# Residual products of a decoder layer as two matmuls over 64 rows of the array each

## The chip, the cores and the metric

One core of one Trainium2 chip runs the whole layer in one launch. The metric is the device time of one execution in microseconds (us).

## The reference

A hybrid decoder layer on 256 tokens of width 2048, batch 1, depth 1, all in float32. Three times a product with a weight matrix is added to the residual stream h:

```python
hn = rmsnorm(h, norm_mix_w[l])
q, k, v, g_ret, xr, yr, g_a, g_b = jnp.split(hn @ w_in[l], offsets, axis=-1)
...
merged = (jax.nn.sigmoid(g_a) * (ret_out @ w_proj_ret[l])
          + jax.nn.sigmoid(g_b) * (rnn_out @ w_proj_rnn[l]))
h = h + merged @ w_mix_out[l]
hn = rmsnorm(h, norm_xa_w[l])
mem_n = rmsnorm(mem, norm_mem_w[l])
h = h + memory_cross_attention(hn, mem_n, xa_w_q[l], xa_w_k[l], xa_w_v[l], xa_w_o[l])
hn = rmsnorm(h, norm_ffn_w[l])
h = h + conv_gated_ffn(hn, ffn_w_up[l], ffn_conv_w[l], ffn_conv_b[l], ffn_w_down[l])
return rmsnorm(h, final_norm_w)
```

memory_cross_attention ends in `o @ w_o` (2048 x 2048), conv_gated_ffn in `(silu(gate) * val) @ w_down` (5632 x 2048).

## The kernel before

Every weight matrix is streamed from HBM once, in chunks of 512 x 512 (KC = 4 k-tiles of 128 rows, BW = 512 columns). A chunk is loaded into `raw` by SyncE's queue, cast to a rounded float32r part `hi` by ScalarE (L210), and its remainder `lo` = raw - hi is formed by VectorE (L211). Activations are split into a high and a low part in the same way (`s` tiles: columns 0 to 255 hold the high part of 256 tokens, 256 to 511 the low part). A product is then three float32r matmuls: high x hi, low x hi, high x lo.

There are two forms of product. gemm_t keeps the weights in the array and streams the activations; its result has features on the partitions (L266). gemm_n keeps 128 tokens of the activations in the array and streams 512 columns of a weight part; its result has tokens on the partitions, `acc[:, tt, :]` with tt = 0, 1 for the two row tiles of 128 tokens (products_n, L276 to L278). One chunk in gemm_n is 2 row tiles x 4 k-tiles x 3 = 24 matmuls, the 12 of tt = 0 first. A block of 512 output columns with 2048 rows of weights has four chunks.

The accumulators come from a pool `pm` of three tiles, each of two PSUM banks (128 x 2 x 512 float32); gemm_t takes two of them, gemm_n one. Small results (transposes, scores, attention) use a second pool `px` of two one-bank tiles.

`plan` lists all products in order, and `chunks` fetches each chunk AHEAD = 2 chunks before use. Work between products is hung on this sequence by `later(n, fn)`, which runs fn n + 1 chunks further on; so transposes of the residual (`turn`, L306) stand between the chunks of the next block. The order on each engine is fixed when the program is built. Work inside `tc.high_priority(URGENT)` is put earlier in it.

The residual products are `residual` (L709; w_mix_out and xa_w_o, four blocks each) and `down` (L838; w_down in three parts of 4, 4 and 3 blocks of hidden features, for each of them four blocks of output columns). Each adds its accumulator to `hrow[b]`, the residual with tokens on the partitions, in one VectorE instruction of 128 x 1024, and ScalarE then squares the rows for the next rmsnorm (`squares`, L725). The last block of the last part of `down` has a form of its own, with two accumulators and halves of 256 columns.

Of the kernel before, what the change touches and what calls it, by code (L numbers as in the profile page):

```python
# [16 lines left out]
P = 128  # L17
D = 2048
S = 256
NT = D // P  # L20
# [7 lines left out]
BW = 512  # L28
KC = 4
KH = 2  # L30
# [4 lines left out]
URGENT = 5  # L35
# [29 lines left out]
def hybrid_layer(  # L65
# [25 lines left out]
    act, dve, pe, pool, sp = nc.scalar, nc.vector, nc.tensor, nc.gpsimd, nc.sync  # L91
# [11 lines left out]
    def nm(s):  # L103
        count[0] += 1
        return f"{s}_{count[0]}"

    def big(shape, dt=F32, s="b"):
        return bp.tile(shape, dt, tag="big", name=nm(s))
# [4 lines left out]
    def acc():  # L113
        return pm.tile([P, 2, BW], F32, tag="acc", name=nm("acc"))
# [48 lines left out]
    b0 = 0  # L163
# [57 lines left out]
    def later(n, fn):  # L221

        pending.append((step[0] + n + 1, fn))

    def chunks(nk, w, row, c):

        w_, row_, nk_, c_ = plan[gemms[0]]
        assert (row_, nk_, c_) == (row, nk, c) and w_.tensor is w.tensor, (gemms[0], row, nk, c)
        gemms[0] += 1
        for k in range(0, nk, KC):  # L230
            prefetch(1)
            (r_, c_), parts = ahead.pop(0)
            assert (r_, c_) == (row + k * P, c)
            prefetch(AHEAD)
            yield k, parts
            step[0] += 1
            due = [p for p in pending if p[0] <= step[0]]
            pending[:] = [p for p in pending if p[0] > step[0]]
            for _, fn in due:
                fn()  # L240

    def gemm_t(w, row, st, nk, col):

        accs = [acc(), acc()]
        first = gemms[0] == 0
        phase = 0
        for k0, parts in chunks(nk, w, row, col):
            last = k0 + KC >= nk
            for pr in range(2):
                if first and k0 == 0:  # L250
                    runs = [[(t, kk, j) for t in (0, 1)] for kk in range(KC) for j in range(2)]
                else:
                    if k0 == 0:
                        phase = 0
                    elif last:
                        phase = 1
                    runs = [[(t, kk, j) for j in range(2) for kk in range(KC)] for t in (phase, 1 - phase)]
                    phase = 1 - phase
                for t, kk, j in (r for run in runs for r in run):
                    k = k0 + kk  # L260
                    sx = st[k // 2][:, k % 2, :]
                    part = parts[kk // KH][t][:, kk % KH, (2 * pr + j) * P : (2 * pr + j + 1) * P]
                    a = accs[pr][:, j, :]
                    if t == 1:
                        a, sx = a[:, S:BW], sx[:, 0:S]
                    pe.matmul(  # L266
                        a, part, sx, start=k == 0 and t == 0, stop=k == nk - 1 and t == 0, skip_group_check=True
                    )
                if pr == 0 and not last:
                    st[(k0 + KC) // 2 + 1]  # L270
        return accs

    def products_n(o, sx, hi, lo, tt, start, stop):
        h = sx[:, tt * P : (tt + 1) * P]
        l = sx[:, S + tt * P : S + (tt + 1) * P]
        pe.matmul(o, h, hi, start=start, stop=False)  # L276
        pe.matmul(o, l, hi, start=False, stop=False)  # L277
        pe.matmul(o, h, lo, start=False, stop=stop)  # L278

    def gemm_n(w, row, st, nk, col):  # L280

        a = acc()
        for k0, parts in chunks(nk, w, row, col):
            for tt in range(2):
                for kk in range(KC):
                    k = k0 + kk
                    hi, lo = (t[:, kk % KH, :] for t in parts[kk // KH])
                    products_n(a[:, tt, :], st[k // 2][:, k % 2, :], hi, lo, tt, k == 0, k == nk - 1)
        return a

    def product(o, l, r, start, stop):

        for i, (a, b) in enumerate(((l[0], r[0]), (l[0], r[1]), (l[1], r[0]))):
            pe.matmul(o, a, b, start=start and i == 0, stop=stop and i == 2, skip_group_check=True)  # L294
# [87 lines left out]
    def rsqrt_small(ap, n, scale, eps):  # L382
        v = sp_.tile([P, n], F32, tag="rv", bufs=4, name=nm("rv"))
        dve.tensor_scalar(out=v, in0=ap, scalar1=scale, scalar2=eps, op0=ALU.mult, op1=ALU.add)
        o = sp_.tile([P, n], F32, tag="ro", bufs=5, name=nm("ro"))
        pool.tensor_tensor(out=o, in0=v, in1=mhalf[:, 0:n], op=ALU.pow)
        return o
# [158 lines left out]
    for g in range(2):  # L546
        dec = big([P, 4, S], s="dec")
        vs, turned = [], []
        for b, o in enumerate((O_Q, O_K)):
            a = qacc if g == b == 0 else gemm_t(w0, 0, xs, NT, o + g * BW)  # L550
# [13 lines left out]
        for b in range(2):  # L564
            a = gemm_n(w0, 0, xs, NT, O_G + g * 1024 + b * BW)
            t = big([P, 2, BW], s="gate")
# [70 lines left out]
    for b in range(4):  # L637
# [4 lines left out]
        for pr, a in enumerate(gemm_t(w0, 0, xs, NT, O_XR + b * BW)):  # L642
            z = scaled(a, "xz")
            for j in range(2):
                t = 4 * b + 2 * pr + j
# [56 lines left out]
    def residual(w, st, out, wcol, steps=None):  # L702

        ss = sp_.tile([P, 2, 4], F32, tag="ss0", name=nm("ss"))
        for b in range(4):
            if steps:
                steps(b)
            h = hrow[b]
            dve.tensor_add(h, h, gemm_n(w, 0, st, NT, b * BW))  # L709
            squares(h, ss, b)  # L710
            for pr in range(2):
                later(pr, lambda b=b, pr=pr: turn(b, pr, out, wcol))
        return ss

    def turn(b, pr, out, wcol):
        for t in transposed(hrow[b][:, :, pr * S : (pr + 1) * S]):
            out.append(split_cols(t, lambda j: wcol(4 * b + 2 * pr + j)))

    def squares(y, ss, i):
        for tt in range(2):  # L720
            square(y[:, tt, :], ss[:, tt, i : i + 1])

    def square(y, o):
        junk = tp.tile([P, BW], F32, tag="tmp", name=nm("junk"))
        act.activation(junk[:, 0 : y.shape[1]], y, AF.Square, accum_out=o)  # L725
# [16 lines left out]

    h1s = []
    ss1 = residual(w_mix_out[0], merged, h1s, p_xa, memory_steps)


# [65 lines left out]

    h2s = []
    ss2 = residual(xa_w_o[0], osp, h2s, p_ffn)
    rs2 = rstd_rows(ss2)
    later(1, lambda: spread_tokens(rs2))
# [15 lines left out]
    def down(b0, hid, b, final):  # L832

        n = len(hid) * 2
        h = hrow[b]
        if not final or b < 3:
            a = gemm_n(ffn_w_down[0], b0 * BW, hid, n, b * BW)
            dve.tensor_add(h, h, a)  # L838
            if final:
                finish(b)  # L840
            return
        accs = [acc(), acc()]
        parts = [p for _, ps in chunks(n, ffn_w_down[0], b0 * BW, b * BW) for p in ps]
        for tt in range(2):
            for c in range(2):
                cs = slice(c * S, (c + 1) * S)
                for k in range(n):
                    hi, lo = (t[:, k % KH, cs] for t in parts[k // KH])
                    products_n(accs[c][:, tt, 0:S], hid[k // 2][:, k % 2, :], hi, lo, tt, k == 0, k == n - 1)
                dve.tensor_add(h[:, tt, cs], h[:, tt, cs], accs[c][:, tt, 0:S])  # L850
                square(h[:, tt, cs], ss3[:, tt, b + c : b + c + 1])
            part = sp_.tile([P, 1], F32, tag="pt3", bufs=2, name=nm("pt3"))
            dve.tensor_reduce(out=part, in_=ss3[:, tt, 0:4], axis=AX.X, op=ALU.add)
            dve.tensor_scalar(out=part, in0=part, scalar1=1.0 / D, scalar2=EPS, op0=ALU.mult, op1=ALU.add)
            r = rsqrt_small(ss3[:, tt, 4:5], 1, 1.0 / D, part)
            for c in (3, 0, 1, 2):
                y = hrow[c][:, tt, :]
                if c == 3:
                    dve.scalar_tensor_tensor(
                        out=y, in0=y, scalar=r, in1=wfin[1][:, 1, :], op0=ALU.mult, op1=ALU.mult  # L860
                    )
                elif c == 1:
                    dve.tensor_scalar_mul(y, y, r)
                else:
                    act.mul(y, y, r)
                sp.dma_start(out=out[0, tt * P : (tt + 1) * P, c * BW : (c + 1) * BW], in_=y)
# [3 lines left out]
    def finish(b):  # L870

        for tt in range(2):
            y = hrow[b][:, tt, :]
            square(y, ss3[:, tt, b : b + 1])
            dve.tensor_tensor(out=y, in0=y, in1=wfin[b // 2][:, b % 2, :], op=ALU.mult)

    b0 = 0
    for part, nb_ in enumerate(FF_PARTS):
        final = part == len(FF_PARTS) - 1
        hid = []  # L880
# [11 lines left out]
        if final:  # L892
            wfin = []
            for i in range(2):
                t = big([P, 2, BW], s="wf")
# [43 lines left out]
```

## Time and profile before

| | |
|---|---|
| median of 3 runs | 2056.66 us (2056.39 to 2058.0) |
| profiled execution, own time | 2058.6 us |
| its span, first to last instruction | 2056.8 us |
| TensorE matmul (PE) busy | 2043.5 us, 10988 matmuls |
| weight loads (PEld) busy | 1771.3 us, 10988 loads |
| VectorE (DVE) busy | 1336.8 us |
| ScalarE (ACT) busy | 1055.4 us |
| mean granted TensorE clock | 0.998 |
| DMA | 392.32 MB, 191 GB/s |

The span is the time that the instructions cover; the execution's own time has 1.8 us more around it. PE and PEld are the two sides of TensorE, the streaming of columns and the loading of the stationary operand, and are recorded apart. Matmuls are pipelined, so records of consecutive ones overlap, and their durations can't be added up. In the views, a line has start, length, engine, line of the kernel, operation, result and operands, and the number of instructions that were merged into it.

### The profile page before, as it was taken

What the parts mean: (1) busy time and instruction counts of PE and PEld (TensorE: products, weight loads), DVE (VectorE), ACT (ScalarE), POOL (GpSimd) and SP (SyncE); (2) the same over time, 40 slices, a digit from 0 to 9 for tenths busy, and PEclk for the clock granted to TensorE, in tenths of its full rate; (3) what the DMA queues carried; (4) which work ended last, traced back from release to release, by engine and by line L of the source; (5) the groups of instructions that cost most, each with busy time, mean ns of one, the idle gap of its engine ahead of it and who ended that gap; (6) DMA issues with size and microseconds to landing.
All of it is one profiled execution on the core that took longest, in us unless ns stands there. A gap on an engine that the chain in (4) does not pass through costs nothing.

```text
span 2056.8 us, 27227 instructions
## 1 busy us (share of the span) xinstructions
PE 2043.5 (99%) x10988; PEld 1771.3 (86%) x10988; DVE 1336.8 (65%) x1682; ACT 1055.4 (51%) x1397; POOL 7.7 (0%) x12
## 2 busy tenths in 40 slices
PE   8999999999999999999999999999999999999998
PEld 7888888888888888888888888888888888888887
DVE  6757658888555555566555555577764777656774
ACT  6545447667444444465444454455543555435553
POOL 0000000000000000000000000000000000000000
PEclk9999999999999999999999999999999999999999
DMA  9554554555655565766555555555655555654663
GB/s 330 199 197 163 186 194 156 192 174 168 205 196 190 168 202 194 249 231 205 172 176 172 177 170 178 184 184 177 208 189 194 181 199 167 214 193 164 203 216 114
DMA packets 200399, 392.32 MB, mean 191 GB/s; under 512 B 6737, under 2 KB 11345, under 8 KB 200273
## 3 DMA queue, kind: packets, MB, share of 16 engines
q1 hardware_dynamic: 199040, 388.42, 56.9%
q10 hardware_dynamic: 1232, 2.16, 0.3%
q8 instruction: 86, 1.41, 0.3%
q14 instruction: 41, 0.33, 0.0%
HBM read 388.46 MB, written 2.10 MB: 190 GB/s over the span
## 4 chain that ended last, share of the span: by engine, by line
PE 97%; DMA 1%; ACT 0%; issue 0%; DVE 0%; SPq 0%; POOL 0%; ACTq 0%; POOLq 0%; DVEq 0%
PE acc L266 61%; PE acc L278 11%; PE acc L277 11%; PE acc L276 11%; PE sm L294 2%; DMA raw<-in_w_in 1%; PE sm L611 1%; PE sm L306 1%; ACT junk L421 0%; ACT hi L210 0%; DVE lo L211 0%; PE sm L778 0%; PE sm L377 0%; SPq L399 0%; SPq L192 0%
## 5 line engine op out<-in xcount | busy, mean ns | idle before, releaser
L211 DVE TENSOR_TENSOR lo<-raw,hi 128x1024 fp32r<-128x1024 f32 (+1 forms) x713 | 854.4, 1221 | 545.8 <-ACT hi L210 485.1
L210 ACT CAST hi<-raw 128x1024 fp32r<-128x1024 f32 x711 | 728.3, 1049 | 713.5 <-PE acc L277 264.5
L266 PE MATMUL acc<-s,hi 128*128 128x512 f32 x3712 | 903.2, 392 | 1.4 <-DVE hi L208 1.3
L266 PEld LDWEIGHTS acc<-s,hi 128*128 128x128 f32 x3712 | 679.0, 189 | 130.4 <-ACT s L350 1.6
L266 PEld LDWEIGHTS acc<-s,lo 128*128 128x128 f32 x3712 | 487.6, 191 | 24.9 <-DVE lo L211 1.6
L266 PE MATMUL acc<-s,lo 128*128 128x256 f32 x3712 | 500.1, 283 | 0.5 <-DVE lo L211 0.5
L276 PE MATMUL acc<-hi,s 128*128 128x512 f32 (+1 forms) x1016 | 392.1, 386 | 0.0
L277 PE MATMUL acc<-hi,s 128*128 128x512 f32 (+1 forms) x1016 | 391.2, 385 | 0.0
L278 PE MATMUL acc<-lo,s 128*128 128x512 f32 (+1 forms) x1016 | 391.2, 385 | 0.0
L277 PEld LDWEIGHTS acc<-hi,s 128*128 128x128 f32 x1016 | 191.4, 188 | 38.0 <-DVE s L328 0.5
L278 PEld LDWEIGHTS acc<-lo,s 128*128 128x128 f32 x1016 | 191.2, 188 | 37.8
L276 PEld LDWEIGHTS acc<-hi,s 128*128 128x128 f32 x1016 | 191.4, 188 | 37.4
L316 ACT COPY c<-acc 128x512 f32<-128x512 f32 x116 | 67.0, 579 | 108.8 <-PE acc L266 108.8
L317 DVE TENSOR_TENSOR uz<-acc,c 128x512 f32<-128x512 f32 x44 | 30.3, 688 | 27.3 <-ACT c L316 27.3
L827 DVE SCALAR_TENSOR_TENSOR fv<-uz,pf,fv 128x255 f32<-128x255 f32 (+1 forms) x88 | 38.5, 480 | 7.8 <-ACT fv L825 7.4
L827 DVE SCALAR_TENSOR_TENSOR fg<-uz,pf,fg 128x255 f32<-128x255 f32 (+1 forms) x88 | 38.5, 480 | 7.8 <-ACT fg L825 7.4
L825 ACT ACTIVATE fg<-uz,pf 128x256 f32<-128x256 f32 x44 | 24.1, 595 | 18.5 <-DVE uz L436 18.5
L825 ACT ACTIVATE fv<-uz,pf 128x256 f32<-128x256 f32 x44 | 24.1, 597 | 16.3 <-DVE uz L436 16.3
L350 ACT ACTIVATE s<-sm,pb 128x256 fp32r<-128x256 f32 x48 | 21.7, 471 | 18.3 <-DVE s L351 18.3
L436 DVE TENSOR_TENSOR uz<-uz,rsb 128x512 f32<-128x512 f32 x44 | 30.3, 689 | 0.7
L725 ACT ACTIVATE junk<-nat 128x512 f32<-128x512 f32 (+1 forms) x26 | 15.4, 593 | 25.1 <-DVE nat L709 11.2
L351 DVE SCALAR_TENSOR_TENSOR s<-sm,pb,s 128x256 fp32r<-128x256 f32 x48 | 22.4, 480 | 5.7 <-ACT s L350 5.7
(166 smaller groups left out, 753.0 us busy)
## 6 DMA issues: line engine op xcount, KB each, us to landing
raw<-in_w_in SPq DMA_DIRECT2D x109, 1024.0 KB, 5.1
raw<-in_ffn_w_up SPq DMA_DIRECT2D x88, 1024.0 KB, 5.1
raw<-in_ffn_w_down SPq DMA_DIRECT2D x44, 1024.0 KB, 5.2
raw<-in_w_proj_rnn SPq DMA_DIRECT2D x16, 1024.0 KB, 5.2
raw<-in_w_proj_ret SPq DMA_DIRECT2D x16, 1024.0 KB, 5.2
raw<-in_w_mix_out SPq DMA_DIRECT2D x16, 1024.0 KB, 5.1
raw<-in_xa_w_k SPq DMA_DIRECT2D x16, 1024.0 KB, 5.1
raw<-in_xa_w_q SPq DMA_DIRECT2D x16, 1024.0 KB, 5.1
```

The costliest lines, as they stand in the source:

```text
L210: act.copy(hi[:, ds], raw[:, cs, :])
L211: dve.tensor_tensor(out=lo[:, ds], in0=raw[:, cs, :], in1=hi[:, ds].bitcast(F32), op=ALU.subtract)
L266: pe.matmul(a, part, sx, start=k == 0 and t == 0, stop=k == nk - 1 and t == 0, skip_group_check=True)
L276: pe.matmul(o, h, hi, start=start, stop=False)
L277: pe.matmul(o, l, hi, start=False, stop=False)
L278: pe.matmul(o, h, lo, start=False, stop=stop)
L294: pe.matmul(o, a, b, start=start and i == 0, stop=stop and i == 2, skip_group_check=True)
L316: act.copy(c, a[:, :, S:BW])
L317: dve.tensor_tensor(out=o, in0=a[:, :, 0:S], in1=c, op=ALU.add)
L436: dve.tensor_tensor(out=z, in0=z, in1=rsb2, op=ALU.mult)
L825: act.activation(y, z[:, j, :], AF.Identity, scale=pf[:, 2, t : t + 1], bias=pf[:, 3, t : t + 1])
L827: dve.scalar_tensor_tensor(out=y[:, s:S], in0=z[:, j, 0 : S - s], scalar=pf[:, 2 - s, t : t + 1], in1=y[:, s:S], op0=ALU.mult, op1=ALU.add,)
```

## The change

gemm_r takes the place of gemm_n in the residual products. Each matmul over 128 rows of the array (the 128 values of a k-tile) becomes two over 64 rows, on the two halves of the partitions, one behind the other in the program. The two halves add up in different banks: `accs[tt][:, 0, :]` and `accs[tt][:, 1, :]`. So a block has two accumulator tiles, one for each row tile of tokens, in place of one tile for both. add_rows adds the four banks to the residual with four VectorE instructions of 512 columns, with URGENT priority. In `down` the last block of the last part keeps its form.

```diff
+    HP = P // 2
+
+    def gemm_r(w, row, st, nk, col):
+        accs = [acc(), acc()]
+        for k0, parts in chunks(nk, w, row, col):
+            for tt in range(2):
+                for kk in range(KC):
+                    k = k0 + kk
+                    hi, lo = (t[:, kk % KH, :] for t in parts[kk // KH])
+                    sx = st[k // 2][:, k % 2, :]
+                    h = sx[:, tt * P : (tt + 1) * P]
+                    l = sx[:, S + tt * P : S + (tt + 1) * P]
+                    for i, (a, b) in enumerate(((h, hi), (l, hi), (h, lo))):
+                        for r in range(2):
+                            rows = slice(r * HP, (r + 1) * HP)
+                            pe.matmul(
+                                accs[tt][:, r, :], a[rows], b[rows], start=k == 0 and i == 0,
+                                stop=k == nk - 1 and i == 2, skip_group_check=True,
+                            )
+        return accs
+
+    def add_rows(h, accs):
+        with tc.high_priority(URGENT):
+            for tt in range(2):
+                for r in range(2):
+                    dve.tensor_add(h[:, tt, :], h[:, tt, :], accs[tt][:, r, :])
...
             h = hrow[b]
-            dve.tensor_add(h, h, gemm_n(w, 0, st, NT, b * BW))
+            add_rows(h, gemm_r(w, 0, st, NT, b * BW))
             squares(h, ss, b)
...
         if not final or b < 3:
-            a = gemm_n(ffn_w_down[0], b0 * BW, hid, n, b * BW)
-            dve.tensor_add(h, h, a)
+            add_rows(h, gemm_r(ffn_w_down[0], b0 * BW, hid, n, b * BW))
             if final:
                 finish(b)
             return
```

In the tables and views, the lines of the kernel after are 29 higher from gemm_r on: the matmul of gemm_r is L308, an addition L318.

## The prediction

> **What bounds the kernel now.** I read the page first (busy times, then the chain that ended last), then the groups of instructions, then the timeline of PE and of the weight loads inside one residual product, to get the real pitch of a matmul.
>
> The page, busy times and chain:
>
> ```profile
> span 2056.8 us, 27227 instructions
> PE 2043.5 (99%) x10988; PEld 1771.3 (86%) x10988; DVE 1336.8 (65%) x1682; ACT 1055.4 (51%) x1397; POOL 7.7 (0%) x12
> PE 97%; DMA 1%; ACT 0%; issue 0%; DVE 0%; SPq 0%; POOL 0%; ACTq 0%; POOLq 0%; DVEq 0%
> PE acc L266 61%; PE acc L278 11%; PE acc L277 11%; PE acc L276 11%; PE sm L294 2%; DMA raw<-in_w_in 1%; PE sm L611 1%; PE sm L306 1%; ACT junk L421 0%; ACT hi L210 0%; DVE lo L211 0%; PE sm L778 0%; PE sm L377 0%; SPq L399 0%; SPq L192 0%
> ```
>
> PE is the bound from end to end, and a third of its chain is L276 to L278, the three products of gemm_n. Nothing counts here but the time of matmuls on the array. PEld is busy for 86% of the span while PE is busy for 99%: weight loads already run under matmuls, on all 128 rows. The recorded duration of a matmul is not its price, since the records overlap; the price is the distance between starts. The timeline in the first residual product, PE and then the weight loads:
>
> ```profile
> 870.59 0.39 PE L278 MATMUL acc<-lo,s 128*128 128x512 f32 x1
> ...
> 871.95 0.39 PE L278 MATMUL acc<-lo,s 128*128 128x512 f32 x1
> 872.18 0.60 PE L306 MATMUL sm<-cid,nat 128*128 128x128 f32 x4
> 872.54 0.48 PE L276 MATMUL acc<-hi,s 128*128 128x512 f32 x1
> ```
> ```profile
> 871.50 0.19 PEld L277 LDWEIGHTS acc<-hi,s 128*128 128x128 f32 x1
> 871.73 0.19 PEld L278 LDWEIGHTS acc<-lo,s 128*128 128x128 f32 x1
> 871.95 0.59 PEld L306 LDWEIGHTS sm<-cid,nat 128*128 128x128 f32 x4
> 872.51 0.19 PEld L276 LDWEIGHTS acc<-hi,s 128*128 128x128 f32 x1
> 872.62 0.19 PEld L277 LDWEIGHTS acc<-hi,s 128*128 128x128 f32 x1
> ```
>
> Six pitches between the two L278 lines give (871.95 - 870.59) / 6 = 0.2267 us for 512 columns. Each load starts with the matmul before its own and takes 0.19 us, so it is hidden. The last two loads start 0.11 us apart: the closest pair of full loads in this view, and so a floor for the load path. Two more rows, from where products of 256 columns run:
>
> ```profile
> 150.70 0.28 PE L266 MATMUL acc<-s,lo 128*128 128x256 f32 x1
> 150.82 0.81 PE L294 MATMUL sm<-s,s 128*128 128x256 f32 x6
> ```
>
> 256 columns have a pitch of 0.12 us. 512 columns less 256 are 0.2267 - 0.12 = 0.107 us, so 512 columns stream in 0.213 us, and about 0.0133 us of every matmul is a fixed gap, whatever its columns. That gap is all that PE could give back without doing fewer columns.
>
> **The change, part by part.** The residual products are 4 blocks of w_mix_out, 4 of xa_w_o and 4 + 4 of w_down at 16 k-tiles x 2 row tiles x 3 = 96 matmuls each, and 3 of w_down at 12 x 2 x 3 = 72: 16 x 96 + 3 x 72 = 1752 matmuls, 1752 x 0.2267 = 397 us of PE time. Each becomes two matmuls of 512 columns over 64 rows, first rows 0 to 63, then 64 to 127; in the built program they carry the places (0, 0) and (64, 0) of the array, and write different banks. The columns streamed per matmul stay 512, so the change halves nothing: the best that it can do is to run the two beside each other.
>
> *A pair on PE.* No matmul in the trace uses fewer than 128 rows, so the price of a pair has bounds only. If the array takes them one after the other, it is 2 x 0.2267 = 0.453. If it takes them together, each half of the rows goes through its own matmul and gap, 0.2267, and the pair costs what one did. Two things can move that. Two loads now share a pitch: at 0.11 each that is 0.22, under 0.2267, so they just fit, with 3% to spare. And the second matmul waits for a load that starts late; two starts with two loads on the array cost 2 x 0.12 = 0.24 in the row of 256 columns, which is the upper end of the pair that runs together. I take 0.2267, since disjoint rows, partitions and banks leave nothing for one half to wait for, and the array already does two things at once (a load under a matmul). Ends: 0.22 and 0.24, that is 1752 x (-0.0067 to +0.0133) = -12 to +23 us, and 0 as the value.
>
> The Trainium skill (TensorE: Matmul & The Clock Gate, Measured speedup vs the span model) gives matmuls on separate rows the time of one plus about 4 ns for each further one. By it the pair would be 0.231 and the sum 7 us longer than mine; no run here shows it yet.
>
> *Switches between 128 and 64 rows.* In the built program's order the PE changes the size of its tiles 38 times: into and out of each stretch of residual products, around each group of transposes (line 306) between them, one spread_tokens and one group of softmax products. The trace of before has no such switch; the transposes go in and out at 872.18 without a hole. If a switch is free it costs 0; if it empties the array, the next matmul can't start until the last has ended, 0.39 - 0.227 = 0.16 us; if the load waits as well, another 0.19. So 0 to 38 x 0.35 = 13 us. I take the emptying, 38 x 0.16 = 6 us, as the price that needs nothing but a different shape of the array.
>
> *The additions.* 19 additions of 1024 columns (L709 1.216 us, L838 1.215 us) become 76 of 512 columns; the nearest row, L317 (512 columns, one operand in PSUM), takes 0.688. That is 4 x 0.688 - 1.216 = 1.54 us more on DVE per block, 29 us in all, beside PE: DVE is busy for 65%. What hides it: the first row tile's two additions can start 12 matmuls (2.7 us) before the block's end. After the end two remain, with one lo (L211, 1.22) between them in DVE's order, 2.6 us against 1.2 before. Behind them wait ACT's squares (L725), ACT's hi behind those, and the transposes; these start one chunk (24 matmuls, 5.4 us) after the block. If this cover were gone, 1.4 us would show 19 times, 27 us. I book 0.
>
> *PSUM.* A block now holds two accumulators out of three. The next block's first row tile takes the third; its second needs the old first one, 24 matmuls or 5.4 us after that was finished, and needs two additions and perhaps a lo ahead of them, 2.6 us. 0, with about 2.8 us to spare. Loads by DMA, hi and lo are the same in number and order of use.
>
> Sum against the profiled execution (span 2056.8, own time 2058.6): 0 + 6 + 0 + 0 = +6, so 2064.8. That execution lies 1.9 above the median of the runs; on the median 2056.66 it is **2063 us**. With its ends (-12 + 0, +23 + 13) this case alone spans 2045 to 2093.
>
> **Rivals.**
>
> *Faster: the gap is hidden.* If the gap of 0.0133 belongs to taking over new weights in the same rows, and one half's gap lies under the other half's streaming, the pair costs 0.213 when the two loads run beside each other too, and 0.22 when they don't. 1752 x -0.0133 = -23, or -12; with up to 6 for the switches, 2034 to 2051, say 2040. It decides from a pair under 0.2267 - 6 / 1752 = 0.223. For it: L611's fp32 products of 256 columns (five from 345.93 on in 1.24 us, the last 0.38) start (1.24 - 0.38) / 4 = 0.215 apart, twice 0.107 and nearly no gap, so a gap isn't inevitable. Against it: each half still has new weights for every matmul in its own rows, so its own gap stays; and loads 0.11 apart leave almost no room. 0.25.
>
> *Slower by a tenth: a load waits for the matmul on its own rows.* Then the pair costs its matmul and a load in the open: half to all of the 0.11 that two loads lie apart, so 1752 x 0.055 to 0.11 = +96 to +193, plus 6: 2159 to 2256. The PEld share of 86% under PE's 99% speaks against it for full tiles, and nothing shows it for 64 rows. The Trainium skill (same page, Part 3, "What overlaps and what doesn't") says that a load overlaps a running matmul only on other rows; the trace disagrees for 128 rows, where L277's load (871.50) lies under L276's matmul on the same rows. 0.12.
>
> *The change doesn't do what it says: one after the other.* The pair costs 0.453, 1752 x 0.2267 = +397, plus 6: 2460. For it: the trace has no two matmuls at once, PE's starts are in order, and these are four-byte operands. Against it: the disjoint rows and banks. 0.18.
>
> **How the numbers follow.** The forecast has 0.45: of it 0.28 slower by over 0.2% (4 us, about what a measurement of this kernel can tell from no change), 0.12 within, 0.05 faster. The faster rival: 0.23 faster, 0.02 within. The other two, 0.30, are slower. So 0.28, 0.14, 0.58. Cases of both signs hold 0.70, so the likeliest one's own range, 2045 to 2093, stands beside the whole. The range reaches down to the faster rival's 2034 and up to the waiting load's 2256 with the switches' upper end (13 - 6) on top, 2263; the two that run in order are left out, 0.18.
>
> **What would show it.** PE's instructions grow by 1752 matmuls and as many loads. Right: the starts of the two halves lie at most about 0.06 apart and the pairs 0.22 to 0.24; the windows of the residual products (87 us for w_mix_out) keep their length; around each group of transposes some 0.16 us are lost per switch; DVE grows by about 29 us and no PE idle is put down to an addition. Wrong: starts 0.227 apart throughout (in order), pairs at 0.29 or more (loads in the open), pairs at 0.216 (gap hidden), or PE waiting for DVE at the start of a block.

## The result, and the profile after

The kernel after takes 2063.92 us (median of 7 runs, 2063.24 to 2066.69) against 2057.95 us of before in the same 7 rounds: a ratio of 1.0032, 95% interval 1.0022 to 1.0042, so 4.5 to 8.6 us slower. The page of after, busy times and chain:

```profile
span 2062.3 us, 30767 instructions
PE 2048.3 (99%) x12740; PEld 1767.1 (86%) x12740; DVE 1363.4 (66%) x1739; ACT 1052.0 (51%) x1397; POOL 7.7 (0%) x12
PE 95%; DMA 2%; DVE 1%; ACT 1%; issue 1%; SPq 0%; POOL 0%; ACTq 0%; POOLq 0%; DVEq 0%
PE acc L266 61%; PE acc L308 17%; PE acc L277 4%; PE acc L276 4%; PE acc L278 4%; PE sm L323 2%; DMA raw<-in_w_in 1%; PE sm L640 1%; DVE lo L211 1%; DMA raw<-in_w_mix_out 1%; PE sm L335 1%; ACT hi L210 0%; ACT junk L450 0%; DVE nat L318 0%; PE sm L807 0%
```

PE has 1752 matmuls and 1752 loads more, and is still the bound. L308, the matmuls of gemm_r, stand for 17% of the chain, about 350 us: one after the other, 3504 of them would take 794. The timeline in w_down, PE and then the loads, shows why:

```profile
1510.24 0.62 PE L308 MATMUL acc<-hi,s 64*128 64x512 f32 x4
1510.69 0.39 PE L308 MATMUL acc<-lo,s 64*128 64x512 f32 x2
...
1511.60 0.62 PE L308 MATMUL acc<-hi,s 64*128 64x512 f32 x4
```
```profile
1510.47 0.19 PEld L308 LDWEIGHTS acc<-lo,s 64*128 64x128 f32 x2
1510.69 0.41 PEld L308 LDWEIGHTS acc<-hi,s 64*128 64x128 f32 x4
```

Two matmuls fit into the 0.39 us that the record of one takes: they run beside each other. Six pairs (two of lo and four of hi) lie between 1510.24 and 1511.60, so a pair has a pitch of 1.36 / 6 = 0.2267 us, what one matmul had before. The two loads of a pair also take 0.19 us together, as long as one.

Most of what is lost lies around the transposes. PE of after at the interruption that stands at 872.18 in before:

```profile
876.51 0.39 PE L308 MATMUL acc<-lo,s 64*128 64x512 f32 x2
876.83 0.66 PE L335 MATMUL sm<-cid,nat 128*128 128x128 f32 x4
877.42 0.73 PE L308 MATMUL acc<-hi,s 64*128 64x512 f32 x4
```

From the last pair before to the first pair behind it is 877.42 - 876.51 = 0.91 us; in before, from 871.95 to 872.54, it was 0.59. In all, an interruption by four transposes costs 0.82 us of the products' time, counted over the next eight pairs, where it was 0.475 before: +0.35, or 0.17 for each of its two switches.

The profiled executions differ by up to 4 us in their first 300 us, in which the kernels are alike and wait for first loads. So beside the medians I compare the part from the 601st matmul of L266 (it starts at 302 to 306 us) to the end of the last matmul, read from each run's trace, one trace for each kernel. It is 1744.8 us in before and 1752.4 in after: +7.6.

### The profile page after: what moved, and what is told of

Read it like the earlier page. It is cut to its first block, busy times and chain, and to the rows that moved or that the text cites. A ratio compares the mean times of both kernels' runs of the same rounds, so it can differ in the third digit from the quotient of the medians.

```text
span 2062.3 us, 30767 instructions
## 1 busy us (share of the span) xinstructions
PE 2048.3 (99%) x12740; PEld 1767.1 (86%) x12740; DVE 1363.4 (66%) x1739; ACT 1052.0 (51%) x1397; POOL 7.7 (0%) x12
## 4 chain that ended last, share of the span: by engine, by line
PE 95%; DMA 2%; DVE 1%; ACT 1%; issue 1%; SPq 0%; POOL 0%; ACTq 0%; POOLq 0%; DVEq 0%
PE acc L266 61%; PE acc L308 17%; PE acc L277 4%; PE acc L276 4%; PE acc L278 4%; PE sm L323 2%; DMA raw<-in_w_in 1%; PE sm L640 1%; DVE lo L211 1%; DMA raw<-in_w_mix_out 1%; PE sm L335 1%; ACT hi L210 0%; ACT junk L450 0%; DVE nat L318 0%; PE sm L807 0%
## 5 line engine op out<-in xcount | busy, mean ns | idle before, releaser
L266 PE MATMUL acc<-s,hi 128*128 128x512 f32 x3712 | 902.3, 391 | 1.1 <-DVE hi L208 1.0
L266 PEld LDWEIGHTS acc<-s,hi 128*128 128x128 f32 x3712 | 677.9, 188 | 131.2 <-issue 1.7
L266 PEld LDWEIGHTS acc<-s,lo 128*128 128x128 f32 x3712 | 486.9, 191 | 26.0 <-DVE lo L211 2.9
L266 PE MATMUL acc<-s,lo 128*128 128x256 f32 x3712 | 499.7, 283 | 1.3 <-DVE lo L211 1.2
L308 PE MATMUL acc<-hi,s 64*128 64x512 f32 x2336 | 362.3, 388 | 0.0
L308 PEld LDWEIGHTS acc<-hi,s 64*128 64x128 f32 x2336 | 217.4, 184 | 48.8 <-issue 2.4
L308 PE MATMUL acc<-lo,s 64*128 64x512 f32 x1168 | 227.5, 386 | 0.0
L276 PE MATMUL acc<-hi,s 128*128 128x512 f32 (+1 forms) x432 | 163.3, 378 | 0.0
L277 PE MATMUL acc<-hi,s 128*128 128x512 f32 (+1 forms) x432 | 163.1, 378 | 0.0
L278 PE MATMUL acc<-lo,s 128*128 128x512 f32 (+1 forms) x432 | 163.0, 377 | 0.0
L308 PEld LDWEIGHTS acc<-lo,s 64*128 64x128 f32 x1168 | 109.4, 184 | 23.5
L276 PEld LDWEIGHTS acc<-hi,s 128*128 128x128 f32 x432 | 81.3, 188 | 15.1 <-issue 0.4
L278 PEld LDWEIGHTS acc<-lo,s 128*128 128x128 f32 x432 | 81.3, 188 | 15.0
L277 PEld LDWEIGHTS acc<-hi,s 128*128 128x128 f32 x432 | 81.3, 188 | 14.7
L318 DVE TENSOR_TENSOR nat<-nat,acc 128x512 f32<-128x512 f32 x76 | 51.9, 683 | 10.3 <-PE acc L308 9.7
L754 ACT ACTIVATE junk<-nat 128x512 f32<-128x512 f32 (+1 forms) x26 | 15.6, 599 | 73.5 <-DVE nat L318 64.1
```

Source lines behind the costliest of these rows:

```text
L266: pe.matmul(a, part, sx, start=k == 0 and t == 0, stop=k == nk - 1 and t == 0, skip_group_check=True)
L308: pe.matmul(accs[tt][:, r, :], a[rows], b[rows], start=k == 0 and i == 0, stop=k == nk - 1 and i == 2, skip_group_check=True,)
L318: dve.tensor_add(h[:, tt, :], h[:, tt, :], accs[tt][:, r, :])
```

## The experiments

Three theories for the 6 us were set against each other: the switches between tiles of 128 and 64 rows (38 of them), the additions with their second accumulator (19 blocks), and the pairs themselves (1752). "Rest" is the part behind start-up just described. A ratio is to the runs of before in the same rounds as the kernel.

| kernel | pairs | switches | median us, runs | ratio to before (95%) | rest us |
|---|---|---|---|---|---|
| before | 0 | 0 | 2057.95, 7 | | 1744.8 |
| after | 1752 | 38 | 2063.92, 7 | 1.0032 (1.0022 to 1.0042) | 1752.4 |
| adds_only | 0 | 0 | 2058.13, 11 | 1.0003 (0.9994 to 1.0012) | 1744.9 |
| down_only | 984 | 6 | 2058.95, 11 | 1.0007 (0.9999 to 1.0016) | 1745.8 |
| mix_xo_only | 768 | 32 | 2063.35, 6 | 1.0031 (1.0020 to 1.0043) | 1751.0 |
| half | 876 | 146 | 2093.24, 4 | 1.0172 (1.0158 to 1.0185) | 1779.6 |
| merged_before | 0 | 0 | 2057.75, 11 | 0.9996 (0.9987 to 1.0004) | 1744.7 |
| merged_after | 1752 | 26 | 2063.22, 11 | 1.0026 (1.0017 to 1.0035) | 1750.0 |
| threes | 1752 | 38 | 2066.62, 1 | | 1752.3 |
| one_half | none | 38 | 2065.22, 1 | | 1751.5 |
| twelves | 1752 | 38 | 2253.37, 1 | | 1940.2 |
| twentyfours | 1752 | 38 | 2365.81, 1 | | 2053.5 |

**adds_only.** The additions and the second accumulator without the pairs:

```diff
-                        for r in range(2):
-                            rows = slice(r * HP, (r + 1) * HP)
-                            pe.matmul(accs[tt][:, r, :], a[rows], b[rows], start=k == 0 and i == 0, ...)
+                        pe.matmul(accs[tt][:, k % 2, :], a, b, start=k < 2 and i == 0, ...)
```

> 128 rows as before, but with two accumulators per block (even and odd k-tiles in different banks) and four additions of 512 columns: no pair, no switch of tile size. If the switches make the 6 us (0.17 us each, 38 of them): no more than 1 us above before, the share of late additions. If the additions and the second accumulator make it (6 / 19 = 0.3 us per block): +6 us. If the pairs themselves make it (6 / 1752 = 0.0034 us each): 0.

Measured: the same as before, by the median (+0.2 against before's 2057.94 in its own rounds) and by the rest (+0.1). The 28 us more on DVE (1364.4 against 1336.8) are hidden, and so is the tighter pool of accumulators. The second theory falls, but for one thing that this run can't test: VectorE's order here isn't that of after, and PE waits for none of its additions, where after has two late ones (below).

**down_only and mix_xo_only.** gemm_r and add_rows in one of the two places, gemm_n and one addition in the other.

> gemm_r in down alone (w_down), gemm_n and one addition in residual: 984 pairs, 6 switches, 11 of 19 blocks. Switches: +1.0 us above before. Additions: 11 x 0.3 = +3.5. Pairs: 984 x 0.0034 = +3.4.

> gemm_r in residual alone (w_mix_out and xa_w_o), gemm_n in down: 768 pairs, 32 switches, 8 of 19 blocks. Switches: 32 x 0.17 + 0.7 = +6.1 us above before. Additions: 8 x 0.3 = +2.5. Pairs: 768 x 0.0034 = +2.6.

Measured: the rest grows by 1.0 us with 984 pairs and 6 switches, and by 6.2 us with 768 pairs and 32 switches; the medians by 1.0 and 5.4. More pairs with fewer switches cost less: the pairs aren't the cause, and the switches' numbers hold. That down_only comes out at just 6 x 0.17 is luck, though. When the starts of its matmuls are set one by one against those of before, each of its switches costs 0.24 us (the last one, into products of 256 columns, 0.19), 1.4 in all. And 0.4 comes back, because before loses that once in w_down's third part. There PE waits for the low part of an activation, which VectorE makes behind two lo (PE, then VectorE):

```profile
1994.41 0.61 PE L276 MATMUL acc<-hi,s 128*128 128x512 f32 x2
1995.06 0.50 PE L277 MATMUL acc<-hi,s 128*128 128x512 f32 x1
```
```profile
1992.05 2.36 DVE L211 TENSOR_TENSOR lo<-raw,hi 128x1024 fp32r<-128x1024 f32 x2
1994.32 0.69 DVE L328 SCALAR_TENSOR_TENSOR s<-fo,s 128x512 fp32r<-128x512 f32 x1
```

In down_only one lo stands there, and PE doesn't wait; nor does it in after. adds_only, mix_xo_only and merged_before have the same pause as before.

Together the two parts give 7.2 of after's 7.6; the other 0.4 is a late addition that after has and mix_xo_only hasn't.

**half.** In each chunk the first row tile of tokens on 64 rows, the second on 128:

```diff
+                    if tt == 0:
                         for i, (a, b) in enumerate(((h, hi), (l, hi), (h, lo))):
                             for r in range(2):
...
+                    else:
+                        for i, (a, b) in enumerate(((h, hi), (l, hi), (h, lo))):
+                            pe.matmul(accs[tt][:, k % 2, :], a, b, start=k < 2 and i == 0, ...)
```

> In gemm_r the first row tile of tokens on 64 rows, the second on 128 (even and odd k-tiles in two banks): 876 pairs, 146 switches, the additions as in after. Switches at 0.17 us: 25 us and up to 1 us of late additions above before, about 2083. Additions: +6. Pairs: +3.

Measured: +35 us by the median, +34.8 by the rest, with half the pairs. The direction is that of the switches alone; the size was expected 10 us too small. 35 / 146 = 0.24 us for a switch. The timeline at one, PE and then the loads:

```profile
1513.73 0.39 PE L309 MATMUL acc<-lo,s 64*128 64x512 f32 x2
1514.05 0.73 PE L315 MATMUL acc<-hi,s 128*128 128x512 f32 x2
1514.62 0.40 PE L315 MATMUL acc<-lo,s 128*128 128x512 f32 x1
```
```profile
1514.04 0.30 PEld L315 LDWEIGHTS acc<-hi,s 128*128 128x128 f32 x2 [0.35 <-issue]
1514.38 0.19 PEld L315 LDWEIGHTS acc<-lo,s 128*128 128x128 f32 x1
```

The first load on the new tile size starts at 1514.04, with the first matmul on it, and not 0.227 us earlier, under the last matmul of the old size, as in a stream. So the next start comes after 0.32 us instead of 0.227 (+0.09). The second matmul's load is late too: the next two pitches take 1514.62 - 1514.05 = 0.57 us instead of 0.453 (+0.12). Some 0.03 goes in the next matmuls. Around the transposes the price is lower, because before had already lost a part of it there: in its timeline a second load follows 0.11 us behind the first, at 872.62, and its matmul starts 872.85 - 872.54 = 0.31 us behind the one before it (+0.09):

```profile
872.85 0.40 PE L277 MATMUL acc<-hi,s 128*128 128x512 f32 x1
```

**merged_before and merged_after.** The transposes of both halves of a block at the same chunk border, in either form:

```diff
-            for pr in range(2):
-                later(pr, lambda b=b, pr=pr: turn(b, pr, out, wcol))
+            later(1, lambda b=b: [turn(b, pr, out, wcol) for pr in range(2)])
```

> The kernel before, with both groups of transposes of a residual block put at the same chunk border (later(1) for both): six interruptions of the products fewer, no switch in either form. Each interruption of before lost 0.475 us of which four transposes are 0.436; so 6 x 0.04 = 0.2 us less, the same as before for a measurement.

> The same edit in after: 26 switches in place of 38, pairs and additions unchanged. Switches at 0.17 us: 12 x 0.17 = 2 us less than after, 2062, and the part behind the first 600 matmuls of line 266 shorter than after's by 2 us (a part that start-up doesn't touch). Pairs or additions: as after, 2064.

Measured: the edit alone does nothing (-0.1 in the rest). With the pairs it takes 2.4 us off the rest. Matmul by matmul, 2.0 of it are the six interruptions fewer at 0.35, so 0.17 for each of 12 switches. The two late additions of after are gone as well (0.7), and about 0.4 is lost anew at one place, around 947.5, whose cause I don't know. The medians (2063.22 against 2063.92, from different rounds, where 2062 was expected) couldn't have settled 2 us. It doesn't bring after below before.

**threes.** Does the pair need its order in the program?

```diff
-                    for i, (a, b) in enumerate(((h, hi), (l, hi), (h, lo))):
-                        for r in range(2):
+                    for r in range(2):
+                        rows = slice(r * HP, (r + 1) * HP)
+                        for i, (a, b) in enumerate(((h, hi), (l, hi), (h, lo))):
```

> In gemm_r the three products of rows 0 to 63 first, then the three of rows 64 to 127: the same matmuls, banks, switches and additions, but neighbours in the order mostly share their rows. If PE starts matmuls in their order and only neighbours on different rows overlap, six take 4 pitches in place of 3: 584 x 0.227 = +133 us above after, about 2197. If the order doesn't matter to PE: 2064. If the halves can't overlap behind each other: 2064 + 397 = 2461.

Measured: as after, 1752.3 in the rest. The case of starts in program order is out by 133 us. PE of threes at the same place:

```profile
1510.28 0.62 PE L308 MATMUL acc<-hi,s 64*128 64x512 f32 x4
1510.73 0.40 PE L308 MATMUL acc<-lo,s 64*128 64x512 f32 x2
1510.96 0.62 PE L308 MATMUL acc<-hi,s 64*128 64x512 f32 x4
```

Although the built program has hi, hi, lo on one half and then hi, hi, lo on the other, they run in pairs at 0.2267 us, so the second half's hi starts beside the first half's. In the records the two starts of a pair lie 10 ns apart, 3 to 4 in after.

**one_half.** The same with rows 0 to 63 alone (`for r in range(1)` in gemm_r and add_rows).

> Leaves out all matmuls and additions of rows 64 to 127, so the residual products lack half of their sums: 1752 single matmuls on 64 rows, 38 switches. If a half has a full matmul's time and the other half ran wholly beside it: the residual stretches as long as in after, 2064 (up to 1 us less for the two late groups of transposes). If the partner cost something, or half the rows stream faster: shorter by 1752 times that, 0.013 each if the fixed gap went, 23 us.

```profile
1510.01 0.61 PE L308 MATMUL acc<-hi,s 64*128 64x512 f32 x2
1510.47 0.39 PE L308 MATMUL acc<-lo,s 64*128 64x512 f32 x1
1510.69 0.61 PE L308 MATMUL acc<-hi,s 64*128 64x512 f32 x2
```

Measured: three single matmuls take 1510.69 - 1510.01 = 0.68 us, 0.2267 each, and the rest is 0.9 us shorter than after's, about the share of late additions. A matmul on half the rows has the full price, gap included, and its partner is free.

**twelves and twentyfours.** How far apart may partners stand? The loop over r is put outside that over kk (twelves), or outside that over tt (twentyfours).

> As threes, but twelve matmuls of rows 0 to 63 (a row tile of tokens in a chunk), then twelve of rows 64 to 127. If each half of the rows takes its own matmuls as they come, as far ahead as twelve: 2064, the part behind the first 600 matmuls of line 266 at 1752 as in after. If PE looks only a few matmuls ahead (three were within reach): up to 22 pitches for 12 pairs, 1752 x 10 / 12 x 0.227 = +331 us, about 2395.

> The same with all 24 matmuls of a chunk on rows 0 to 63 first, then 24 on the others. Within reach: 2064. With a reach of w matmuls under 24 the halves share only part of the time: between 2064 and 1752 x 22 / 24 x 0.227 = +364 us, 2428; the trace then shows how many start beside the other half.

Measured: +188 and +301 us in the rest. PE of twelves in w_down:

```profile
1701.32 0.84 PE L308 MATMUL acc<-hi,s 64*128 64x512 f32 x4
1701.89 0.50 PE L308 MATMUL acc<-lo,s 64*128 64x512 f32 x2
1702.12 0.62 PE L308 MATMUL acc<-hi,s 64*128 64x512 f32 x2
1702.58 0.39 PE L308 MATMUL acc<-lo,s 64*128 64x512 f32 x1
1702.82 0.61 PE L308 MATMUL acc<-hi,s 64*128 64x512 f32 x2
1703.27 0.39 PE L308 MATMUL acc<-lo,s 64*128 64x512 f32 x1
1703.28 0.83 PE L308 MATMUL acc<-hi,s 64*128 64x512 f32 x4
```

A period of twelve matmuls takes 1703.28 - 1701.32 = 1.96 us, 8.6 pitches, so 3.4 matmuls had a partner's pitch for nothing. Four hi and two lo start in its first 0.80 us. Since each half goes hi, hi, lo, these are the last three of one half and the first three of the other, side by side; six more follow alone. In twentyfours the excess per chunk is 301 / 73 = 4.1 us (19 blocks have 73 chunks), 18.2 pitches. Of 48 matmuls 48 - 24 - 18.2 = 5.8 are shared, at two changes of half, so again about three at each. So one half gets about three matmuls ahead of the program's order, however long the stretch; that is enough for threes.

## Why the prediction was right or wrong, point by point

*The bound.* Right: PE is busy for 99% after as before, and the change is what PE's pitches and switches make of it.

*The pair, 0 us.* Right in its value: the pitch is 0.2267 us in the timeline, and the rest of 984 pairs in down_only grows by 1.0 us, less than the 1.4 of its 6 switches. Half of the reason was wrong. I took the loads to share a path, with 3% to spare; the two loads of a pair run beside each other, two in 0.19 us, so the lower end of 0.22 had no ground. What holds the pair at 0.2267 is the full pitch of each half's own matmul, gap included, which one_half shows alone. The 4 ns that the Trainium skill (TensorE: Matmul & The Clock Gate, Measured speedup vs the span model) gives for a second matmul stands in after as the distance of the two starts (3 to 4 ns); in a stream it isn't added to the pair, whose pitch would then be 0.231.

*The switches, 38 x 0.16 = 6 us.* Right in kind, and near in size for a half-right reason. I took the emptying of the array, 0.16, as the price, and the late load, 0.19 more, only for the upper end; half shows 0.24 for a switch in a stream of 512 columns, 0.09 for the first start and 0.12 for the second load, and the trace of after 0.17 where transposes had cost a part of it already. Nor do the runs show the emptying as I drew it: the first start comes 0.32 behind the last, before that one's record of 0.39 is over. And at 872.18 the trace of before wasn't without a hole, since its second matmul comes 0.09 late. The sum over after, matmul by matmul against before: 13 interruptions by four matmuls at 0.35 to 0.39 and one by the softmax products at 0.38 make 4.9; the ten borders of the five stretches at 0.24 (the last 0.19) make 2.4. That is 7.3 for 38 switches, 0.19 each. The term was 1 us too small, and that it meets the 6.0 between the medians so closely is luck.

*The additions, 0 us.* Nearly right. In most blocks the cover holds, and adds_only loses nothing. In two blocks of w_mix_out in after it doesn't: PE waits for the last addition and loses 0.25 and 0.44 us, which I had listed as a sign against the forecast. VectorE before the second of them:

```profile
888.62 1.40 DVE L318 TENSOR_TENSOR nat<-nat,acc 128x512 f32<-128x512 f32 x2
891.81 1.22 DVE L211 TENSOR_TENSOR lo<-raw,hi 128x1024 fp32r<-128x1024 f32 x1 [1.79 <-ACT hi L210]
892.95 0.68 DVE L318 TENSOR_TENSOR nat<-nat,acc 128x512 f32<-128x512 f32 x1
893.55 1.22 DVE L211 TENSOR_TENSOR lo<-raw,hi 128x1024 fp32r<-128x1024 f32 x1
894.68 0.68 DVE L318 TENSOR_TENSOR nat<-nat,acc 128x512 f32<-128x512 f32 x1
```
```profile
894.85 0.33 PE L335 MATMUL sm<-cid,nat 128*128 128x128 f32 x1
895.42 0.55 PE L335 MATMUL sm<-cid,nat 128*128 128x128 f32 x3 [0.24 <-DVE nat L318]
```

I counted a lo ahead of an addition by its 1.22 us, but not what it waits for. The two halves' additions are apart in VectorE's order, and the lo between them waits for a hi (1.79 us idle), which stands behind a square (L754) in ScalarE's order, which waits for the first two additions. The last addition ends 6.7 us after the first began. In the groups, ScalarE's wait for additions grew from 14.5 us (L709 and L838 together) to 64.1, hidden but for these two:

```profile
L754 ACT ACTIVATE junk<-nat 128x512 f32<-128x512 f32 (+1 forms) x26 | 15.6, 599 | 73.5 <-DVE nat L318 64.1
```

4.9 + 2.4 + 0.7 is 8.0; less the 0.4 that before loses in w_down and after doesn't, it is 7.6, the whole of the rest. That the medians differ by 6.0 and the rest by 7.6 lies within the interval of the former, 4.5 to 8.6.

*The rivals.* The gap isn't hidden: one half alone has it, and the loads that were to stand in the way don't. No load waits for a matmul on its own rows: the loads at 1510.47 lie under matmuls of both halves, so the rule of the Trainium skill (same page, Part 3, "What overlaps and what doesn't") that they overlap only on other rows doesn't hold for 64 rows either. One after the other doesn't happen in the order of after; twentyfours shows what three quarters of it costs.

## What to carry to other kernels

Splitting a full matmul (here float32r, 512 columns, new weights each time) into two on half the rows costs and gains nothing by itself when PE is the bound: each half has the full pitch, and both run at once, as long as the partners stand within about three matmuls of each other in the program. What counts then is how often the stream changes its tile size, 0.24 us each time in a stream of 512 columns and 0.17 around the transposes, so work on 64 rows belongs in long stretches with nothing on 128 rows between. When a VectorE instruction is cut into several, look at what the scheduler puts between the pieces, and at what that waits for.

## What the runs showed that I had not expected

PE doesn't start matmuls strictly in the program's order when they are on different rows: in threes they pair up over a distance of three, and in twelves and twentyfours each half runs about three matmuls ahead. The Trainium skill (TensorE: Matmul & The Clock Gate, Part 3, "What overlaps and what doesn't") has matmuls in program order in start and end; these runs disagree for the starts of tiles on different rows. Two loads on different rows take the 0.19 us of one.
